# A trunk of two layers on one core: the preparation of mixing weights moved to other steps, operands of the late token sums loaded earlier, and the preparation of query and key weights moved to a later stage

## The chip, the cores and the metric

One core of one Trainium2 chip runs the whole program in one launch. The metric is device time in microseconds (us); lower is better.

## The reference, cut to what matters

The program is a trunk of two layers over 1024 tokens of width 1024, all in fp32. The stage in question is layer 0: a token mixer that joins a gated spatial unit and a gated delta rule, with an output projection, and after it an MLP.

```python
hn = rms_norm(h, ln_mix_e[i])
proj = hn @ w_in_e[i]
a_uv, b_qkv, b_z, b_beta, b_a = jnp.split(proj, split_at, axis=-1)
a_out = gmlp_spatial_gate(jax.nn.gelu(a_uv), gmlp_v_gain[i], gmlp_ws[i], gmlp_bs[i])
b_out = gated_deltanet(b_qkv, b_z, b_beta, b_a, ...)
h = h + jnp.concatenate([a_out, b_out], axis=-1) @ w_out_e[i]
hn = rms_norm(h, ln_mlp[layer])
h = h + jnp.square(jax.nn.relu(hn @ w_mlp1[layer])) @ w_mlp2[layer]
```

`gated_deltanet` splits the tokens into chunks of 64, solves a unit lower triangular system for each chunk and head, and then carries a state through the chunks one after the other (the recurrence). Layer 1 has differential attention with the weights `w_qkv_o` in the mixer's place; those weights are prepared during layer 0.

## The kernel before, in words

**Number format.** Each fp32 operand of a large product is split into two fp32r parts, hi (a cast on ACT) and lo (a subtraction on DVE), and a product is hi·hi + lo·hi + hi·lo: three matmuls (`mm3`). A split of a 128x512 piece is so one ACT cast and one DVE subtraction. Weights pass from DRAM into `raw` slots by SP's queue and are then split.

**Layer 0's mixer** (`even_mix`). Fifteen projections are cut into 384 steps. `pump(n)` runs the steps up to number n between the pieces of the solver and the recurrence, so that TensorE (PE) always has matmuls to do while these wait: steps 108 to 170 beside keys, decay and systems (`system`), 36 beside `solve`, 25 beside `merge`, 29 behind it, and 194 beside the recurrence. What an engine does first is decided when the program is built; on the chip each engine works through its list in order, and an instruction that waits holds up all behind it. That holds for the queues too: SP issues nearly all loads and stores, and POOL those of the preparations.

`solve` (L2292 on) works on DVE: 30 pairs of small operations, `outer` (L2315) and `work` (L2316), and then a transpose that gives `dt` (L2326), in slot "B". The first product that needs it is `py`. The diagonal blocks come in by `work<-diag` and other blocks by `ay<-am_dram`, on SP.

**The output projection** (`mix_seven`, L1669) is one level of a fast scheme with seven products instead of eight: the weight is cut into 2x2 quarters, the tokens' features likewise, and sums of quarters are multiplied. Each product is 48 matmuls of 128x512. The weight combinations are prepared ahead by `prepare_mix` (L300): 28 units, seven for each of four k, each with loads of `w_out`, sums on DVE, a split into a tile `wm` in slot "B", and stores to `mix_dram`. `pump` calls for the next unit at steps after 260 whose number is a multiple of 4 (`BEFORE = 260`). A unit's two stores are held back in a list (`late`) until the next unit begins. Slot "B" is one buffer, so a unit's cast waits until the stores of the unit before have been done.

The token sums are made in `put_ab` (L2167). The first half of the tokens, as it is made, is kept in `halves` in DRAM; for the second half, `halves` is loaded back into temporaries (`tmp`, four buffers) and t1 = first half - second half, t2 = the other quarter - t1 and, later, t4 are made; t2 goes through `t2_dram` (in the trace `t_dram`). t3 (the difference of two quarters) is made at the beginning of `mix_seven` from loads of `halves`. `second_gates` gives the second half's gated values: `guv` is loaded from `uv_dram`, which the last projection steps write; then come the products with the spatial weights (`pgm`), 16 gate operations on DVE (`guv`, L2138) and transposes (`pab`).

Inside `mix_seven`, the third product and the gates come first, then products 1, 5, 6, 7, 2, 4. Finished rows are added to `acc` and stored to `h_dram` by SP (L1706). After product 2's first strip, `rms` (far) sends the reciprocal norms through DRAM: `rd` and then `rb`, a broadcast row, on SP's queue; the normalised operands of the MLP (L1768 to L1773) are made in product 4. `prepare` (L236) makes the query and key weights: 32 units, each with two loads, a cast, a subtraction and two stores to `qk_dram`, all queued on POOL. Five units are called in `mix_seven`, the other 27 in the MLP's second product (`product2`), beside its own products 2, 4, 5 and 7.

The scalar `lame` (in `attn_consts`) comes from a load of `diff_lambda` on SP and an exponential on ACT; it stands between the mixing and the MLP.

## Time and profile before

| | us |
|---|---|
| median of 3 runs | 2576.97 |
| lowest, highest | 2575.22, 2578.17 |
| profiled execution | 2580.56 |
| its span in the trace | 2578.8 |
| PE busy | 2482.0 |
| granted clock of PE, mean | 0.98 |

The profiled execution is 1.8 us longer than its span, and 3.6 us above the median. In the trace, a row of a timeline is start, duration, engine, line, operation, output<-input, and in brackets the idle time before it and what ended it. The chain of waits goes back from the last instruction, each step to what released it. Where a name stands for several buffers, numbers are left out. In the trace, the last matmul of the projections ends at 372.14, the mixing at 525.33, and the MLP's first matmul starts at 551.02.

### The profile page before, as it was taken

How to read it: one execution, taken by the hardware profiler on the slowest of the kernel's cores; microseconds unless marked ns; L12 is line 12 of the kernel's file. 1: busy time of each engine (PE TensorE's matmuls, PEld its weight loads, DVE VectorE, ACT ScalarE, POOL GpSimd, SP SyncE). 2: the span in 40 equal slices, each digit the busy share in tenths (PEclk: the TensorE clock that was granted, in tenths of full speed). 3: DMA queues.
4: the chain of work that ended last, by engine and by line, in shares of the span. 5: the costliest groups of instructions: out<-in, count | busy, mean ns of one | idle time of the engine just before them, and what ended most of it. 6: DMA issues, size and time to landing. Idle time of an engine off the chain costs nothing.

```text
span 2578.8 us, 39762 instructions
## 1 busy us (share of the span) xinstructions
PE 2482.0 (96%) x13369; PEld 2105.7 (82%) x13369; DVE 1888.3 (73%) x3654; ACT 1362.3 (53%) x2768; POOL 378.2 (15%) x491
## 2 busy tenths in 40 slices
PE   9999984869999999999999999999999999999999
PEld 7898983748778888787889999998788888888887
DVE  7877764468886787776795777877788666877676
ACT  5635571246555644563462777765564555445452
POOL 0212441020111120241111233230000000000000
PEclk9999996979999999999999999999999999999999
DMA  8465677655877896798544222266457547756651
GB/s 244 125 182 139 208 241 238 224 181 185 306 266 256 313 326 185 244 314 262 196 135 156 91 67 75 74 217 208 164 188 253 188 168 267 234 182 192 203 176 65
DMA packets 339862, 511.76 MB, mean 198 GB/s; under 512 B 52324, under 2 KB 155720, under 8 KB 339656
## 3 DMA queue, kind: packets, MB, share of 16 engines
q1 hardware_dynamic: 318104, 441.56, 52.7%
q0 software_dynamic: 20992, 67.13, 7.6%
q8 instruction: 105, 1.72, 0.3%
q14 instruction: 101, 0.83, 0.1%
q10 hardware_dynamic: 560, 0.53, 0.1%
HBM read 343.40 MB, written 165.68 MB: 197 GB/s over the span
## 4 chain that ended last, share of the span: by engine, by line
PE 83%; DMA 5%; DVE 5%; issue 4%; ACT 1%; POOL 1%; SPq 0%; DVEq 0%; POOLq 0%; ACTq 0%
PE mm L83 72%; PE po L83 3%; PE qk L83 2%; PE tr L86 2%; PE aux L83 2%; DMA raw<-in_w_mlp_dram 1%; DVE w L375 1%; DMA mix_dram<-wm 1%; DVE raw L449 1%; DMA uv_dram<-t 1%; DMA gate_dram<-w 0%; DMA gd<-g 0%; DVE g L449 0%; DVE lg L1478 0%; DMA t<-halves 0%
## 5 line engine op out<-in xcount | busy, mean ns | idle before, releaser
L83 PE MATMUL mm<-hi,w 128*128 128x512 f32 x1920 | 626.8, 401 | 58.2 <-ACT w L371 25.7
L83 PE MATMUL mm<-g,w 128*128 128x512 f32 x2592 | 601.6, 394 | 3.1 <-DVE g L375 2.5
L83 PEld LDWEIGHTS mm<-g,w 128*128 128x128 f32 x2592 | 486.6, 188 | 116.9 <-DVE g L375 2.9
L371 ACT CAST w<-raw 128x512 fp32r<-128x512 f32 x518 | 315.2, 617 | 373.1 <-PE mm L83 258.8
L83 PEld LDWEIGHTS mm<-hi,w 128*128 128x128 f32 x1920 | 365.4, 191 | 146.8 <-ACT w L371 26.1
L375 DVE TENSOR_TENSOR w<-raw,w 128x512 fp32r<-128x512 f32 x518 | 350.0, 684 | 163.1 <-ACT w L371 126.9
L83 PE MATMUL mm<-w,hi 128*128 128x256 f32 (+2 forms) x2112 | 438.8, 302 | 1.6 <-ACT t L2078 0.8
L83 PE MATMUL mm<-lo,w 128*128 128x512 f32 x960 | 383.9, 400 | 1.7 <-DVE lo L375 1.0
L83 PEld LDWEIGHTS mm<-w,hi 128*128 128x128 f32 x2112 | 339.0, 189 | 18.7 <-DVE k L1388 1.3
L83 PE MATMUL mm<-w,lo 128*128 128x256 f32 (+2 forms) x1056 | 316.2, 300 | 0.0
L83 PE MATMUL mm<-t,w 128*128 128x512 f32 x1152 | 273.2, 396 | 1.9 <-DVE g L449 1.9
L83 PEld LDWEIGHTS mm<-t,w 128*128 128x128 f32 x1152 | 217.6, 189 | 53.0 <-issue 2.4
L83 PEld LDWEIGHTS mm<-lo,w 128*128 128x128 f32 x960 | 183.6, 191 | 44.1 <-DVE lo L375 2.2
L83 PEld LDWEIGHTS mm<-w,lo 128*128 128x128 f32 x1056 | 199.4, 189 | 8.2
L371 ACT CAST g<-graw 128x512 fp32r<-128x512 f32 x216 | 132.9, 617 | 38.0 <-DMA graw<-gd 20.4
L375 DVE TENSOR_TENSOR g<-graw,g 128x512 fp32r<-128x512 f32 x216 | 147.2, 684 | 7.5 <-ACT g L371 3.7
L416 POOL TENSOR_TENSOR r<-ms,mhalf 128x4 f32<-128x4 f32 x12 | 17.2, 1431 | 797.4 <-DVE ms L414 767.1
L1481 ACT ACTIVATE lg<-lg,nm 128x128 f32<-128x128 f32 (+7 forms) x128 | 99.3, 776 | 39.4 <-DVE nm L1478 38.3
L518 ACT ACTIVATE g<-g 128x512 f32<-128x512 f32 x100 | 63.0, 631 | 74.6 <-DVE g L449 74.3
L1478 DVE CUSTOM_DVE_ANT_0 lg<-qk,al 128x512 f32<-128x512 f32 (+3 forms) x128 | 74.1, 586 | 19.1 <-PE qk L83 17.1
L83 PE MATMUL mm<-ohi,w 128*128 128x512 f32 x256 | 83.8, 400 | 0.3 <-DVE acc L1821 0.3
L519 ACT ACTIVATE g<-g 128x512 f32<-128x512 f32 x128 | 80.5, 631 | 2.2
(412 smaller groups left out, 3774.6 us busy)
## 6 DMA issues: line engine op xcount, KB each, us to landing
raw<-in_w_mlp_dram SPq DMA_DIRECT2D x352, 256.0 KB, 3.7
graw<-gd SPq DMA_DIRECT2D x224, 256.0 KB, 3.4
gd<-g SPq DMA_DIRECT2D x192, 256.0 KB, 3.6
acc<-h_dram SPq DMA_DIRECT2D x64, 256.0 KB, 4.7
qk_dram<-w POOLq DMA_DIRECT2D x64, 256.0 KB, 5.5
keep<-in_w_mlp_dram SPq DMA_DIRECT2D x64, 256.0 KB, 5.1
w<-qk_dram SPq DMA_DIRECT2D x64, 256.0 KB, 4.3
raw<-in_w_in_e_dram SPq DMA_DIRECT2D x60, 256.0 KB, 3.8
```

The source lines that it names most:

```text
L83: self._next(self.engine.matmul(*a, **k))
L86: self._next(self.engine.transpose(*a, **k))
L371: inst = self.nc.scalar.copy(hi, src)
L375: inst = (lo_engine or self.nc.vector).tensor_tensor(lo, src, f32(hi), ALU.subtract)
L416: nc.gpsimd.tensor_tensor(r, ms, self.mhalf[:, 0:4], ALU.pow)
L449: nc.vector.tensor_tensor(out, a, b, op)
L518: nc.scalar.activation(g, src, AF.Relu)
L519: nc.scalar.activation(g, g, AF.Square)
L1478: nc.vector.tensor_tensor_reduce(out=lg[:, k0:k1], in0=ps[:, : k1 - k0], in1=al[:, u0 + k0 : u0 + k1], scale=-0.5 ** (hd + 1), scalar=3.0e ...
L1481: nc.scalar.activation(lg[:, :n], lg[:, :n], AF.Exp, bias=nm[:, r, nch - 1 : nch], scale=-1.0, accum_out=me.sums[:, b, r : r + 1])
```

## The change

The units of `prepare_mix` are called at other steps: every eighth from 100 to 188, and every eighth from 240 to 376 (30 calls). Each unit stores its two parts at once in one store of 512 KB. On DVE (`wm` are the units' tiles, `w` those of the projections, `outer` and `work` the solver's) a piece in the middle of the solve was, before:

```order
L2316 TENSOR_TENSOR work_331_1865<-work_331_1865,outer_337_1885 128x11x20
L2315 TENSOR_TENSOR outer_337_1885<-work_331_1865 128x210
L2316 TENSOR_TENSOR work_331_1865<-work_331_1865,outer_337_1885 128x10x21
L2315 TENSOR_TENSOR outer_337_1885<-work_331_1865 128x198
L2316 TENSOR_TENSOR work_331_1865<-work_331_1865,outer_337_1885 128x9x22
L2315 TENSOR_TENSOR outer_337_1885<-work_331_1865 128x184
L375 TENSOR_TENSOR w_352_2096<-raw_350_2093,w_351_2095 128x512
L2316 TENSOR_TENSOR work_331_1865<-work_331_1865,outer_337_1885 128x8x23
L375 TENSOR_TENSOR w_357_2167<-raw_355_2164,w_356_2166 128x512
L2315 TENSOR_TENSOR outer_337_1885<-work_331_1865 128x168
L375 TENSOR_TENSOR w_363_2232<-raw_361_2229,w_362_2231 128x512
```

and is now:

```order
L2313 TENSOR_TENSOR work_344_1915<-work_344_1915,outer_350_1935 128x16x15
L369 TENSOR_TENSOR wm_352_1956<-wm_332_1801,wm_352_1956 128x512
L2312 TENSOR_TENSOR outer_350_1935<-work_344_1915 128x240
L313 TENSOR_TENSOR wm_332_1801<-wm_332_1801,t_351_1954 128x512
L2313 TENSOR_TENSOR work_344_1915<-work_344_1915,outer_350_1935 128x15x16
L313 TENSOR_TENSOR wm_331_1800<-wm_331_1800,wm_332_1801 128x512
L2312 TENSOR_TENSOR outer_350_1935<-work_344_1915 128x238
L2313 TENSOR_TENSOR work_344_1915<-work_344_1915,outer_350_1935 128x14x17
L2312 TENSOR_TENSOR outer_350_1935<-work_344_1915 128x234
L2313 TENSOR_TENSOR work_344_1915<-work_344_1915,outer_350_1935 128x13x18
L2312 TENSOR_TENSOR outer_350_1935<-work_344_1915 128x228
L369 TENSOR_TENSOR wm_358_2031<-t_351_1954,wm_358_2031 128x512
```

Four operations of units stand between the solver's pairs, where the projections' alone stood. From the first `outer` to `dt` there were seven other operations and there are now eighteen.

On POOL (`wm` in DRAM is `mix_dram`, `r`, `rd`, `rb` belong to the norm, `fo`, `rv` to recurrence and gates) the end of the units, the mixing, and what follows was, before:

```order
L307 DMA mix_dram_2840<-wm_649_4091 128x512 x2
L307 DMA mix_dram_2840<-wm_659_4147 128x512 x2
L307 DMA mix_dram_2840<-wm_675_4270 128x512 x2
L307 DMA mix_dram_2840<-wm_680_4320 128x512 x2
L307 DMA mix_dram_2840<-wm_684_4368 128x512
L314 DMA wm_635_4017<-in_w_out_e_dram 128x512
L307 DMA mix_dram_2840<-wm_684_4368 128x512
L307 DMA mix_dram_2840<-wm_690_4415 128x512 x2
L352 DMA mix_dram_2840<-wm_698_4471 128x512 x2
L416 TENSOR_TENSOR r_899_5407<-ms_898_5405,mhalf_89 128x4
L245 DMA raw_917_5479<-in_w_qkv_o_dram 128x2x128 x2
L245 DMA raw_920_5488<-in_w_qkv_o_dram 128x2x128 x2
```

and is now:

```order
L307 DMA mix_dram_1115<-wm_686_4354 128x2x512
L2475 TENSOR_TENSOR fo_733_4608<-so_732_4603,mhalf_89 128x4
L2481 TENSOR_TENSOR qkv_450_2842<-qkv_450_2842,qkv_158_703 128x4x128
L2475 TENSOR_TENSOR fo_808_4957<-so_807_4952,mhalf_89 128x4
L2481 TENSOR_TENSOR qkv_450_2842<-qkv_450_2842,qkv_158_703 128x4x128
L2475 TENSOR_TENSOR fo_850_5177<-so_849_5172,mhalf_89 128x4
L2107 TENSOR_TENSOR rv_666_4166<-var_664_4152,mhalf_89 128x8
L2107 TENSOR_TENSOR rv_670_4206<-var_668_4192,mhalf_89 128x8
L2481 TENSOR_TENSOR qkv_450_2842<-qkv_450_2842,qkv_158_703 128x4x128
L1700 DMA h_dram_93<-acc_741_4658 128x512 x4
L1700 DMA h_dram_93<-acc_832_5039 128x512 x4
L1700 DMA h_dram_93<-acc_802_4888 128x512 x2
```

The last fourteen stores of units stood straight ahead of the norm, with loads of the query and key weights (`in_w_qkv_o`) behind it; now the last unit's store stands ahead of eight operations of recurrence and gates, and stores of `h_dram` come next.

Further: t3 is made in `put_ab` as `halves` is written, with a load of the other quarter, and kept in `t3_dram`; `mix_seven` loads it after product 1. The halves for t1 and t2 are loaded at the beginning of `mix_seven` into free slots of hs tiles (`hi0k`, `lo0k`), and t2 is loaded into slots `c0` to `c3` instead of temporaries. Stores of `h_dram` in `mix_seven` and the norm's `rd` and `rb` go on POOL's queue. All 32 units of `prepare` stand in the MLP's second product: product 7 takes six instead of four, and product 4 eleven instead of eight. What follows is the diff, without the lines that only pass arguments on.

```diff
@@
 KA = (6,5)
 ACC = "A2", "A0", "A1", "A3"
 NQK = 112
-BEFORE = 260
+BESIDE = (*range(100, 190, 8), *range(240, 384, 8))
 MARKS = ((224, NQK),)
 TAIL = 210
 FILLA, FILLB, FILLC, FILLD = 62, 36, 25, 29
@@
 
         nc = self.nc
         self.mix_dram = self.dp.tile([7, 4, 2, P, HT], F32, name="mix_dram")
-        late = []
 
         def put(n, k, src):
-            for out, t in late:
-                nc.gpsimd.dma_start(out, t)
-            late.clear()
             both = self.slot("B", [P, 2, HT], F32R, "wm")
-            for j, t in enumerate(self.split(src, both[:, 0], both[:, 1])):
-                late.append((self.mix_dram[n - 1, k, j], f32(t)))
+            self.split(src, both[:, 0], both[:, 1])
+            nc.gpsimd.dma_start(self.mix_dram[n - 1, k].rearrange("j p m -> p j m"), f32(both))
 
         def get(t, j, l, k):
             nc.gpsimd.dma_start(t, w[(4 * j + k) * P : (4 * j + k + 1) * P, l * HT : (l + 1) * HT])
@@
             if k < 3:
                 x, y = pair(k + 1)
             yield
-        for out, t in late:
-            nc.gpsimd.dma_start(out, t)
 
     def mm3(self, ps, a, b, first, last, more=False):
 
@@
         self.r[half], self.rb[half] = self.rms(half, self.sqs[half], ms, rows, far)
         self.hs[half] = self.hs_new[half]
 
-    def rms(self, half, sqs, ms=None, rows=True, far=False, pt=None):
+    def rms(self, half, sqs, ms=None, rows=True, far=False, pt=None, queue=None):
 
 
         nc = self.nc
@@
         rb = None
         if rows and far:
             d = self.dp.tile([4, P], F32, name=self.nm("rd"))
-            nc.sync.dma_start(d.rearrange("t p -> p t"), r)
+            (queue or nc.sync).dma_start(d.rearrange("t p -> p t"), r)
             rb = self.sp.tile([P, HT], F32, tag=f"rb{half}", name=self.nm("rb"), bufs=1)
-            nc.sync.dma_start(rb, d.rearrange("t p -> (t p)").partition_broadcast(P))
+            (queue or nc.sync).dma_start(rb, d.rearrange("t p -> (t p)").partition_broadcast(P))
         elif rows:
             rb = self.row(half, r)
         return r, rb
@@
             for kt in range(NK):
                 if kt in beside:
                     beside[kt]()
-                if n in (2, 4) and kt % 2 or n == 5 and kt > 2 and kt % 2 or n == 7 and kt in (6, 9, 12, 15):
+                if n in (2, 4) and kt % 2 or n == 5 and kt > 2 and kt % 2 or n == 7 and kt > 4 and kt % 2 or n == 4 and kt in (4, 8, 12):
                     next(side, None)
                 a = self.parts(left(n, kt), nc.vector)
                 raw = self.slot(f"c{next(raws)}", [P, HT], F32, "graw")
@@
             nc.sync.dma_start(h_dram[m, :, cols], res[m])
 
 
-    def mix_seven(self, h_dram, gain_next, gates, halves, t1s, t2s, side):
+    def mix_seven(self, h_dram, gain_next, gates, halves, raws, t1s, t2s, t3_dram):
 
         nc = self.nc
         R = range(4)
@@
             nc.vector.tensor_tensor(t, t, ps, ALU.add)
             if done:
                 self.add_square(h, t)
-                nc.sync.dma_start(h_dram[m, :, h * HT : (h + 1) * HT], t)
+                nc.gpsimd.dma_start(h_dram[m, :, h * HT : (h + 1) * HT], t)
 
         def third():
             a[3] = load(3)
@@
             a[5] = load(5)
 
         a = {}
-        t3s = []
         for k in R:
-            u, v = self.tmp(), self.tmp()
-            nc.sync.dma_start(u, halves[k])
-            nc.sync.dma_start(v, halves[4 + k])
-            nc.vector.tensor_tensor(u, v, u, ALU.subtract)
-            t3s.append(self.split(u, *self.hs_parts(0, k)))
+            for j in range(2):
+                t = self.hp.tile([P, HT], F32, tag=f"{('hi', 'lo')[j]}0{k}", name=self.nm("r"))
+                nc.sync.dma_start(t, halves[4 * j + k])
+                raws[j].append(t)
         for n, _ in enumerate(third()):
             if n > 1:
                 next(gates, None)
@@
             yield from product(q, a[1], self.mixed[1][0:4], x[q], True)
             add(q, 1, x[q])
         a[6] = load(6)
+        t3s = []
+        for k in R:
+            t = self.tmp()
+            nc.sync.dma_start(t, t3_dram[k])
+            t3s.append(self.split(t, *self.hs_parts(0, k)))
         for q in R:
             y = bank("aux")
             yield from product(q, a[5], t1s, y, True)
@@
             y = bank("sc")
             yield from product(q, a[2], self.mixed[1][4:], y, True)
             if q == 0:
-                self.rb[0] = self.rms(0, self.sqs[0], far=True)[1]
+                self.rb[0] = self.rms(0, self.sqs[0], far=True, queue=nc.gpsimd)[1]
             add(q, 1, y, True)
         self.x0 = [acc(m, 0) for m in range(KT)]
-        next(side, None)
-        next(side, None)
         for q in R:
             yield from product(q, a[4], t4s, x[q])
             if q == 0:
@@
                     nc.scalar.copy(hi, t)
                     lows.append(nc.vector.tensor_tensor(lo, t, f32(hi), ALU.subtract).ins.name)
             add(4 + q, 1, x[q], True)
-        for _ in range(3):
-            next(side, None)
         self.sqs_last = self.sqs[1]
         self.x1 = [acc(m, 1) for m in range(KT)]
 
@@
 
         halves = self.dp.tile([KT, P, HT], F32, name="halves")
         t2_dram = self.dp.tile([4, P, HT], F32, name="t2_dram")
-        t1s, t2s = [], []
+        t3_dram = self.dp.tile([4, P, HT], F32, name="t3_dram")
+        t1s, t2s, raws = [], [], ([], [])
         self.t4s = []
 
         def put_ab(hf, k, pt):
@@
                 t = self.tmp()
                 nc.scalar.copy(t, flat(pt))
                 nc.sync.dma_start(halves[k], t)
+                if k < 4:
+                    u = self.tmp()
+                    nc.sync.dma_start(u, halves[4 + k])
+                    nc.vector.tensor_tensor(u, u, flat(pt), ALU.subtract)
+                    nc.sync.dma_start(t3_dram[k], u)
             if hf or k > 3:
                 self.mixed[hf][k] = self.split(flat(pt), *self.hs_parts(hf, k))
             if hf and k < 4:
-                u, v = self.tmp(), self.tmp()
-                nc.sync.dma_start(u, halves[k])
+                u, v = raws[0][k], raws[1][k]
                 nc.vector.tensor_tensor(u, u, flat(pt), ALU.subtract)
                 t1s.append(self.split(u, *self.hs_parts(1, 4 + k)))
-                nc.sync.dma_start(v, halves[4 + k])
                 nc.vector.tensor_tensor(v, v, u, ALU.subtract)
                 t2s.append(self.split(v, *self.hs_parts(0, 4 + k)))
                 nc.sync.dma_start(t2_dram[k], v)
             elif hf:
-                u = self.tmp()
+                u = self.slot(f"c{k - 4}", [P, HT], F32, "t2")
                 nc.sync.dma_start(u, t2_dram[k - 4])
                 nc.vector.tensor_tensor(u, flat(pt), u, ALU.subtract)
                 self.t4s.append(self.split(u, *self.hs_parts(1, k - 4)))
@@
                 done += 1
                 if done % 5 == 0:
                     next(rest_of_x, None)
-                if done > BEFORE and done % 4 == 0:
+                if done in BESIDE:
                     next(parts, None)
             self.pe.fill = False
 
@@
                 T.new_hs()
                 for _ in T.mix_out(0, lambda m: acc_of(m, 0), w_out_o[0], h_dram, gain[4], KA[0]):
                     pass
+            side = iter(()) if layer else T.prepare(w_qkv_o[0])
             if layer:
                 for _ in T.mix_out(1, lambda m: acc_of(m, 1), w_out_o[0], h_dram, gain[4], KA[1]):
                     pass
```

More of the change, by code (lines that the diff above doesn't have):

```diff
@@ L1864, in normed, with even_mix @@
         return a
-    def even_mix(self, first, rows_of_rest, rest_of_x, w_in, ws, bs, conv, a_log, dt_bias, v_gain, o_gain, masks, w_out, gain_next, h_dram, side):
+    def even_mix(self, first, rows_of_rest, rest_of_x, w_in, ws, bs, conv, a_log, dt_bias, v_gain, o_gain, masks, w_out, gain_next, h_dram):
         nc = self.nc
@@ L2492, in mixing @@
             self.new_hs()
-            seven.append(self.mix_seven(h_dram, gain_next, second_gates(), halves, t1s, t2s, side))
+            seven.append(self.mix_seven(h_dram, gain_next, second_gates(), halves, raws, t1s, t2s, t3_dram))
             yield from iter(lambda: next(seven[0]), True)
@@ L2672, in trunk @@
         rest = T.load_x(x1, 1, gain[0], h_dram)
-        side = T.prepare(w_qkv_o[0])
-        T.even_mix(first, rows_of_rest, rest, w_in_e[0], gmlp_ws[0], cols[:, 96:100], conv, gdn_a_log[0], gdn_dt_bias[0], gmlp_v_gain[0], gdn_out_gain[0], masks, w_out_e[0], gain[1], h_dram, side)
+        T.even_mix(first, rows_of_rest, rest, w_in_e[0], gmlp_ws[0], cols[:, 96:100], conv, gdn_a_log[0], gdn_dt_bias[0], gmlp_v_gain[0], gdn_out_gain[0], masks, w_out_e[0], gain[1], h_dram)
         T.attn_consts(attn_q_gain[0], attn_k_gain[0], diff_lambda[0], attn_sub_gain[0], lam_init)
```

## The prediction

> **What bounds the kernel now.** I read the page first. TensorE (PE) is the engine that sets the end:
>
> ```profile
> PE 2482.0 (96%) x13369; PEld 2105.7 (82%) x13369; DVE 1888.3 (73%) x3654; ACT 1362.3 (53%) x2768; POOL 378.2 (15%) x491
> ```
>
> PE works 2482 of 2578.8 us. So only its 97 idle us, and matmuls that run at half clock, can be won; whatever another engine saves while PE is busy is worth nothing. The table by stretches shows where the rest lies (columns: length, then busy us of PE, PEld, DVE, ACT, POOL, the granted clock, the DMA share):
>
> ```profile
> 190.00:372.14 182.14, 178.27 (x1515) 166.94 (x1513) 134.48 (x297) 106.57 (x271) 66.86 (x81) 0.98 0.60 187
> 372.14:411.15 39.01, 18.46 (x85) 14.70 (x85) 17.47 (x43) 15.01 (x35) 9.63 (x13) 0.69 0.84 284
> 411.15:442.81 31.66, 13.05 (x35) 8.18 (x33) 14.32 (x23) 6.79 (x12) 4.85 (x9) 0.57 0.74 238
> 442.81:491.38 48.57, 48.56 (x206) 39.04 (x206) 24.43 (x38) 8.97 (x15) 0.00 (x0) 0.96 0.75 257
> 491.38:525.33 33.95, 25.66 (x104) 20.54 (x104) 11.29 (x19) 6.06 (x10) 6.85 (x9) 0.85 0.44 138
> 525.33:551.02 25.69, 0.00 (x0) 0.00 (x1) 18.88 (x36) 11.37 (x21) 6.14 (x11) 0.56 0.66 230
> ```
>
> I cut it where the timeline of PE shows a boundary: the projections end at 372.14, the first of the late products (a[1]) starts at 411.15, the mixing ends at 525.33, the MLP starts at 551.02. From 372.14 to 551.02 PE is busy 105.7 of 178.9 us: 73 of the 97 idle us lie in this one stage. No other engine is full there either (DVE 17 of 39 us); it is a stage of waits. The timeline of PE and the chain of waits say which:
>
> ```profile
> 371.86 0.28 PE L83 MATMUL mm<-w,lo 128*128 128x256 f32 x1
> ...
> 436.38 0.77 PE L83 MATMUL mm<-hi,w 128*128 128x512 f32 x1 [9.56 <-DVE t L2177]
> ...
> 499.67 0.77 PE L83 MATMUL mm<-hi,w 128*128 128x512 f32 x1 [8.29 <-issue]
> ```
>
> ```profile
> 387.54 7.67 DMA uv_dram<-t
> ...
> 395.60 7.29 DMA guv<-uv_dram
> ...
> 440.01 2.76 DMA w<-mix_dram
> ...
> 480.28 11.11 PE mm L83 x48
> ...
> 499.67 6.20 PE mm L83 x16
> ```
>
> First comes a round trip of the last uv tile through memory (15 us), then loads of `halves` for the t1 operands, then the load of the last `mix_dram` unit (440.01 to 442.77). At 436.38 PE waited 9.56 us behind a subtraction that a load of `halves` held up; at 499.67 it waited 8.29 us for the t2 loads. The 48 matmuls in 11.11 us give the price of one product, 0.2315 us a matmul; the 16 matmuls in 6.20 us after the pause at 499.67 should have taken 3.70, so a restart costs 2.5 us of half clock beside the wait. The Trainium skill ("TensorE: Matmul & The Clock Gate", Part 1: The HAM clock gate) says that full clock comes back after some 3.4 us of activity; by that a restart costs 1.7 us, not 2.5, and the two restarts in the sum below would make it 1.6 us lower. The row shows the longer half-rate stretch.
>
> **The change part by part.** *The mixing, from 372.14 to 525.33 (153.2 us).* The order shows that all 28 units are stored before it, that the t1 raws are loaded into slots of their own, t3 is formed while `halves` is written, and t2 is loaded into a free slot. So the waits at 436.38 (9.56), for `mix_dram` (to 442.77) and at 499.67 (8.29) have nothing left to wait for. What is late next is the chain uv store, guv load, 16 gate multiplications, transposes: it ends where a[1] starts, 39.0 us after the projections' end, and the change does not touch it, except that its two transfers (7.67 and 7.29 us, at a DMA share of 0.84) lose the company of seven stores and loads of units. With these at some 4.5 to 5 each I get a[1] at 34 us after the end of the projections; unhelped, 39; if the load waits longer behind the new loads in SP's queue, 50. Then six products of 48 matmuls at 11.11 us: 66.7. The transposes of the second half and the sum matmuls: 2.6. One restart: 2.5. Small waits that I can't name: 4 (0 to 10). Sum 34 + 66.7 + 2.6 + 2.5 + 4 = 109.8, against 153.2: **a gain of 43**. Ends: 50 + 66.7 + 2.6 + 2.5 + 10 = 132, a gain of 21; 30 + 66.7 + 2.6 + 2.5 + 0 = 102, a gain of 51.
>
> *The start of the MLP (25.69 us of wait).* Here are the DVE and SP rows:
>
> ```profile
> 522.75 1.42 DVE L1768 SCALAR_TENSOR_TENSOR acc<-acc,cols,rb 128x512 f32<-128x512 f32 x2 [11.01 <-DMA rb<-rd]
> ...
> 549.04 0.22 DVE L1326 TENSOR_TENSOR t<-t 128x64 f32<-128x64 f32 x1 [6.23 <-DMA t<-in_diff_lambda_dram]
> ```
>
> ```profile
> 508.01 0.37 SPq L420 DMA_DIRECT2D rd<-r x1
> 518.34 0.32 SPq L422 DMA_DIRECT2D rb<-rd x1
> ...
> 539.58 0.99 SPq L1324 DMA_DIRECT2D t<-in_diff_lambda_dram x1
> ```
>
> The reciprocal norms `rb` come 14.7 us after `rd` is issued; the first weights come late because SP stood behind stores of `h_dram`, and ACT's casts stood behind a scalar that waits for `diff_lambda` until 549. After the change the `h_dram` stores are on POOL, the five units of `prepare` with their loads and stores are gone from here, and the MLP's raw loads follow the mixing's on SP at once. PE has 67 matmuls left after the sums of squares (15.5 us), and from `rd` to the first multiplication it is 14.7 again, with an estimated 2 for mean and reciprocal in front of it and 2 for the first cast and subtraction behind: a wait of 3. Then PE is fed tile by tile by DVE and ACT, which share the eight normalised tiles with the first weights; I put 6 us of gaps there, 1.5 for `diff_lambda`, 0.5 for the clock: 11, against 25.7 + 2.5 (the clock after 551.02, as at 499.67): **a gain of 17** (9 to 24). The Trainium skill ("Trainium Kernel Development and Optimization", Key Constraints) says that queues of SP, ACT and POOL share 16 DMA engines, so that another issuer saves only issue time; by it the move of `rd`, `rb` and the stores to POOL brings `rb` no earlier, and the rows agree: between `rd` and `rb` SP waited 10 us for a transfer. My sum takes nothing for that move.
>
> *The solve, where units now are.* The change puts twelve calls of the preparation at steps 100 to 188, where before there were none. The rows:
>
> ```profile
> 158.65 0.21 DVE L2315 TENSOR_TENSOR outer<-work 128x30 f32<-128x30 f32 x1 [1.35 <-DMA work<-diag]
> ...
> 176.86 0.68 DVE L375 TENSOR_TENSOR w<-raw,w 128x512 fp32r<-128x512 f32 x1
> ...
> 184.19 2.12 DVE L2326 STREAM_TRANSPOSE dt<-work 128x1024 f32<-128x1024 f32 x1
> ```
>
> ```profile
>   DVE dt L2326: 0.4, 1
> ```
>
> ```profile
> 150.78 1.06 SPq L2297 DMA_DIRECT2D work<-diag  x2
> 151.88 3.63 SPq L2301 DMA_DIRECT2D ay<-am_dram  x4
> ```
>
> The single row in the middle is PE's wait at `py`, the first product with the solver's result: 0.4 us, so PE arrives just as `dt` is ready, and the amount of matmuls ahead of it is the same in both orders. Every us that `dt` comes later is idle PE. Before, seven other operations stand between the first outer product and `dt`; after, 18 do: 11 x 0.60 (the starts of neighbouring 0.68 us rows are 0.6 apart) = 6.6. In front of the solve, where DVE has no pause, four more unit operations: 2.4; two of the four `ay` loads now precede `work<-diag` on SP: up to 1.8, I take 1. A unit's cast waits until the last unit's store has landed, because all share slot B; in the solve two units are nine rows apart, about 4.4 us of work:
>
> ```profile
> mix_dram<-wm POOLq DMA_DIRECT2D x56, 256.0 KB, 3.5
> ```
>
> With issue, landing and cast that is 4.7 us or more, so DVE itself waits 0.3 to 3 us at two places: 1.0 in all as the value, 6 as the bound. PE's restart adds 2.5. Sum 6.6 + 2.4 + 1 + 1 + 2.5 = 13.5; **a loss of 13** (4 if DVE's gaps take the units up, 20 with all bounds). The store is one of 512 KB where two of 256 KB were; the trace has no such store, and 3.5 and twice 3.5 us bound its landing. A unit also puts POOL's two AFFINE_SELECTs for the next system behind a store that waits for DVE; I take nothing for it beside the unit operations already counted, since the same order on DVE holds both up, and one landing, 3.5 us, as the other end. In the recurrence (190.00 to 372.14) DVE is busy 134 of 182 us, and 18 calls stand there now where 30 stood before, so I take zero.
>
> *The second product pass.* Five units of `prepare` more stand beside products 7 and 4:
>
> ```profile
> 1057.00:1102.00 45.00, 41.93 (x180) 33.45 (x179) 35.07 (x58) 28.13 (x52) 15.89 (x25) 1.00 0.84 287
> 1146.00:1190.00 44.00, 43.34 (x192) 35.00 (x191) 31.26 (x52) 22.95 (x42) 13.53 (x21) 1.00 0.94 289
> ```
>
> A unit moves 0.75 MB: 2.6 us at 287 GB/s. Two more fit in product 7 (16% of 45 us is free); three more (7.9 us) exceed the 2.6 us free in product 4, and 5 us would be late if nothing were loaded ahead: **a loss of 2** (0 to 6).
>
> *The sum*, against the profiled execution's 2580.6 (span 2578.8 and 1.8 around it): 2580.6 - 43 - 17 + 13 + 2 = 2535.6. That execution lay 3.6 above the median of the runs, so I forecast **2532**.
>
> **The rivals.** *A, the waits move (0.17).* The guv load stands in SP's queue behind loads that wait for slots, and the mixing still ends on memory round trips as in the chain's rows (7.67 and 7.29). For it: they are untouched. Against: the other loads have their data ready. a[1] then starts at +50 and other waits remain: the gain of 43 is 21, the time 2554.
> *B, the MLP's start stays bound (0.10).* `diff_lambda` is issued even later on SP, behind the raws, and ACT's casts stand behind it as until 549.04. The 9.5 us from its issue to its use come back, the time 2541.
> *C, the solve hides the units (0.08).* DVE catches up before `py`, so 4 instead of 13, and the mixing gains 51 and the MLP's start 24: 2508.
> *D, slower (0.05).* Each unit's cast waits for the previous store, and ACT and DVE stand still with it, being in order. If that costs 3.5 us at each of the seven units around the solve (24.5) and at each of the 18 units in the recurrence (63, of which the 48 us of DVE's free time there would hide at most a part, say 10), the loss is 24 + 53 and the net gain is gone: 2532 - 13 + 24.5 + 53 = 2596. It decides from about 1.8 us a unit on top of my sum (45 us / 25 units). Against it: before, more units stood in the recurrence, and PE is busy 178 of 182 us there.
> That the units do not leave the mixing is no rival: the order shows it.
>
> **How the numbers follow.** My own case has 0.60. A measurement of this kernel can tell 0.2%, 5 us, from no change; that is 2571.8 to 2582.1. My case and B and C lie wholly below it, A to all but a few per cent, D above: faster 0.93, same 0.02, slower 0.05. The likeliest gives 2532. The mixing at its bounds alone makes it 2524 to 2554; the solve and the MLP's start at theirs add 16 below and 15 above, the second pass 4 above. They do not all fall on one side, so my case alone has some 2512 to 2556. With C's 2508 and A's 2554, which have their own spread, the range is **2505 to 2560**; D and the outer parts of A and C are left out.
>
> **What the profile would show.** The three PE waits at 436, 442 and 499 gone, and PE near 10 of 10 from a[1] to the mixing's end; the stretch from the projections' end to a[1] 30 to 39 us; mixing 102 to 132 in all; the MLP's first matmul 3 to 15 us after it; a new wait of PE at `py` of about 11 us with `dt` as its releaser and half clock after it; product 4 within 6 us of before. I am wrong if `py` shows no wait or one over 20 us, if PE idles in the recurrence behind `wm` casts, or if a[1] starts over 45 us after the projections.

## The result, and the profile after

The changed kernel takes 2534.27 us, median of 4 runs (2529.96 to 2535.88), against 2576.09 (2568.98 to 2578.17): ratio 0.984, 95% interval 0.9817 to 0.9863. The forecast was 2532 in a range of 2505 to 2560. The profiled execution has a span of 2532.8 us, 46.0 less than before; by the medians it is 41.8, since the profiled execution of the kernel before was a long one. The page after, in its first part and in the row of the late products:

```profile
PE 2478.3 (98%) x13369; PEld 2105.5 (83%) x13369; DVE 1889.8 (75%) x3654; ACT 1361.2 (54%) x2768; POOL 375.7 (15%) x481
...
L83 PE MATMUL mm<-hi,w 128*128 128x512 f32 x1920 | 622.5, 400 | 8.6 <-DMA w<-gate_dram 3.6
```

The number of matmuls is the same; 58.2 us of idle time in front of this group have become 8.6. The stretches of the changed kernel, cut where its PE timeline shows the same boundaries as before (py, the projections' end, the first product a[1], the mixing's end), with columns as before:

```profile
0.00:198.39 198.39, 183.58 (x1163) 164.51 (x1163) 156.11 (x347) 106.92 (x265) 43.60 (x49) 0.99 0.72 215
198.39:392.09 193.70, 187.25 (x1648) 174.66 (x1648) 134.42 (x291) 109.35 (x277) 57.85 (x59) 0.95 0.59 182
392.09:431.81 39.72, 25.71 (x115) 21.07 (x115) 14.44 (x37) 8.88 (x23) 1.40 (x2) 0.79 0.84 296
431.81:501.47 69.66, 69.65 (x314) 56.49 (x312) 42.97 (x70) 21.65 (x36) 8.94 (x15) 1.00 0.71 233
```

The fourth row is the main gain: from a[1] on, PE is busy 69.65 of 69.66 us at full clock, where the same products took 114.2 us before. And the PE timeline shows what is left of waits over 2 us between 100 and 520:

```profile
198.39 1.81 PE L83 MATMUL py<-dt,ay 32*32 32x32 f32 x60 [10.66 <-DVE dt L2323]
246.49 0.33 PE L86 MATMUL pq<-ident,qkv 128*128 128x128 f32 x1 [2.50 <-DVE qkv L2004]
...
405.19 2.08 PE L83 MATMUL pgm<-guv,wT 128*128 128x128 f32 x8 [3.48 <-DVE t L2169]
426.05 3.78 PE L83 MATMUL pgm<-guv,wT 128*128 128x128 f32 x16 [7.62 <-DVE guv L2131]
504.76 0.80 PE L83 MATMUL mm<-hi,w 128*128 128x512 f32 x1 [3.30 <-ACT hi L1767]
```

The waits for the t1 and t2 operands and for `mix_dram` are gone. The wait at `py` is new, with `dt` as its releaser, as foreseen; the wait for `guv` (426.05) has stayed. The stages of all kernels, in us, as the PE timelines give them (the projections' end is the end of the last 128x256 matmul; the rest is the span behind the MLP's first matmul):

| kernel | projections' end | to a[1] | to the mixing's end | MLP's wait | rest |
|---|---|---|---|---|---|
| before | 372.1 | 39.0 | 114.2 | 25.7 | 2027.8 |
| changed | 392.1 | 39.7 | 69.7 | 3.3 | 2028.0 |
| units alone | 390.2 | 29.5 | 81.3 | 24.1 | 2022.1 |
| units late | 379.0 | 44.0 | 97.9 | 4.8 | 2030.3 |
| operands back | 394.1 | 28.3 | 81.0 | 6.5 | 2024.4 |
| prepare back | 391.3 | 39.2 | 69.7 | 20.3 | 2024.2 |
| not in the solve | 393.7 | 39.2 | 69.6 | 3.7 | 2026.4 |
| t3 in slots | 390.4 | 32.2 | 69.9 | 3.6 | 2031.6 |
| slots and no call | 395.0 | 31.2 | 69.9 | 4.5 | 2024.9 |
| SP queue | 392.3 | 37.4 | 69.7 | 2.3 | 2028.1 |
| units on POOL | 393.2 | 36.4 | 69.7 | 3.9 | 2026.8 |
| two stores | 384.4 | 37.3 | 69.7 | 3.8 | 2029.1 |
| slots and SP queue | 390.5 | 32.4 | 70.1 | 2.2 | 2029.8 |
| three edits | 386.2 | 31.8 | 69.9 | 2.3 | 2032.0 |

So 46.0 = 114.2 - 69.7 (44.5) + 25.7 - 3.3 (22.4), less 19.9 at the projections' end, 0.7 to a[1] and 0.2 in the rest. Kernels with one code up to the projections' end (changed, prepare back, SP queue, and but for one slot t3 in slots) differ there by 1.9 us, and the rest, whose code hardly differs, by 10; so a few us are read from the stages and not from the spans.

### The profile page after: what moved, and what is told of

Its sections match the earlier page's. It is cut to its first block, busy times and chain, and to the rows that moved or that the text cites. A ratio compares the mean times of both kernels' runs of the same rounds, so it can differ in the third digit from the quotient of the medians.

```text
span 2532.8 us, 39684 instructions
## 1 busy us (share of the span) xinstructions
PE 2478.3 (98%) x13369; PEld 2105.5 (83%) x13369; DVE 1889.8 (75%) x3654; ACT 1361.2 (54%) x2768; POOL 375.7 (15%) x481
## 4 chain that ended last, share of the span: by engine, by line
PE 82%; issue 5%; DMA 5%; DVE 4%; ACT 1%; POOL 1%; SPq 0%; POOLq 0%; DVEq 0%; ACTq 0%
PE mm L83 72%; PE qk L83 2%; PE po L83 2%; PE tr L86 2%; PE aux L83 2%; DMA mix_dram<-wm 1%; DMA wm<-in_w_out_e_dram 1%; DMA w<-gate_dram 1%; DVE lg L1472 0%; DVE t L2001 0%; DMA t<-halves 0%; DMA t<-in_p_dram 0%; DVE w L369 0%; POOL gate_dram L258 0%; DMA diag<-ring 0%
## 5 line engine op out<-in xcount | busy, mean ns | idle before, releaser
L365 ACT CAST g<-graw 128x512 fp32r<-128x512 f32 x216 | 132.9, 617 | 22.4 <-DMA graw<-gd 7.8
L1475 ACT ACTIVATE lg<-lg,nm 128x128 f32<-128x128 f32 (+7 forms) x128 | 99.2, 776 | 38.5 <-DVE nm L1472 37.4
```

The costliest lines, as they stand in the source:

```text
L365: inst = self.nc.scalar.copy(hi, src)
L1475: nc.scalar.activation(lg[:, :n], lg[:, :n], AF.Exp, bias=nm[:, r, nch - 1 : nch], scale=-1.0, accum_out=me.sums[:, b, r : r + 1])
```

## The experiments

**Which part of the change does it.** Four kernels, run together. The first two move the units alone.

```diff
-BESIDE = (*range(100, 190, 8), *range(240, 384, 8))
+BESIDE = tuple(range(264, 384, 4))
```

> The changed kernel with the units called at the steps of before (every fourth from 264 on), each still with one store. My theory: PE's wait at py (10.66 us) goes and the projections end near 372 instead of 392, but the last units are stored some 50 us into the mixing and PE waits for mix_dram again; about 25 us come back there: near 2540 us (2530 to 2555). Rival, the operands loaded ahead are the whole gain and late units cost nothing: 20 us are won, 2514.

Measured: 2553.04, ratio 0.9912 (0.9893 to 0.9931), 19 us slower than the changed kernel. The direction is my theory's and the time lies in its range, but the size is larger than the value that I gave:

```profile
448.46 0.79 PE L83 MATMUL mm<-hi,w 128*128 128x512 f32 x1 [14.12 <-DMA w<-mix_dram]
```

PE waits 14.12 us at one place for a unit's weights. There is no wait at `py`. But the projections end at 379.0, not at 372, though the steps are those of before: 7 us that I come back to at the two stores.

The kernel before, with the units' new steps and the one store, and nothing else:

```diff
-                if done > BEFORE and done % 4 == 0:
+                if done in BESIDE:
```

> The kernel before with the units' steps and the one store of the changed kernel, and nothing else. My theory: it pays the 20 us in the solve and the recurrence, and gains only the waits for mix_dram (5.7 and 3.5 us) and some transfer time in the mixing, 10 to 15: near 2583 us (2575 to 2592), not faster than before. Rival, the units in the mixing were most of its waits: 25 us faster, 2550.

Measured: 2549.33, ratio 0.9897 (0.9879 to 0.9915): 26 us faster. My theory fell, the rival's number is met. In this kernel t1 and t2 are loaded as before, and the PE timeline shows

```profile
198.71 1.49 PE L83 MATMUL py<-dt,ay 32*32 32x32 f32 x48 [10.63 <-DVE dt L2319]
...
414.59 3.46 PE L83 MATMUL pgm<-guv,wT 128*128 128x128 f32 x16 [4.64 <-DVE guv L2131]
475.59 0.77 PE L83 MATMUL mm<-hi,w 128*128 128x512 f32 x1 [7.15 <-DVE t L2179]
525.05 0.79 PE L83 MATMUL mm<-hi,w 128*128 128x512 f32 x1 [24.08 <-ACT w L364]
```

The price at `py` is whole. But the 9.56 us behind a subtraction of t1 (436.38 before) are gone with the units, with no load ahead. In before's DVE list these subtractions stood among the units' operations, in order, and waited for slow loads:

```profile
431.44 0.69 DVE L2180 TENSOR_TENSOR t<-t,t 128x512 f32<-128x512 f32 x1 [6.40 <-DMA t<-halves]
432.05 0.68 DVE L375 TENSOR_TENSOR wm<-wm,wm 128x512 fp32r<-128x512 f32 x1
432.77 0.69 DVE L317 TENSOR_TENSOR wm<-wm,wm 128x512 f32<-128x512 f32 x1
435.55 0.69 DVE L2177 TENSOR_TENSOR t<-t,pab 128x512 f32<-128x512 f32 x1 [2.09 <-DMA t<-halves]
```

Put the other way round, the kernel with late units, which has all of the change but the moved steps, is some 23 us faster than before by its ratio; the two parts, 26 and 23, bring 41 together and so overlap. Whether the units held the subtractions by their place in DVE's list, by the temporaries that they take from the same ring, or by their transfers was not separated. What remains with the old loads are the 7.15 us for t2 at 475.59.

The changed kernel with the token sums' operands as before:

```diff
-                u, v = raws[0][k], raws[1][k]
+                u, v = self.tmp(), self.tmp()
+                nc.sync.dma_start(u, halves[k])
...
+                nc.sync.dma_start(v, halves[4 + k])
...
-                u = self.slot(f"c{k - 4}", [P, HT], F32, "t2")
+                u = self.tmp()
```

(and t3 again at the start of the mixing)

> The changed kernel with the token sums' operands loaded as before (halves into temporaries for t1 and t2, t3 made at the start of the mixing, t2 through temporaries). My theory: the waits for halves and t2 come back as they were, 9.6 + 8.3 and some 5 of half clock and small ones: near 2557 us (2547 to 2565). Rival, without the units' stores the same loads land in time: 2540 or less.

Measured: 2537.47, ratio 0.9845 (0.9824 to 0.9865), 1 us from the changed kernel and within its interval. My theory fell. The stages say why: the late products are 11 us longer (81.0, with 7.41 us of wait for t2), the MLP's wait 3 us, but a[1] comes 28.3 us behind the projections' end instead of 39.7. What the early loads win is lost again in front; that t3's temporaries take most of it is shown below, with t3 in slots.

The changed kernel with `prepare` where it was:

```diff
+        next(side, None)
+        next(side, None)
         for q in R:
             yield from product(q, a[4], t4s, x[q])
...
+        for _ in range(3):
+            next(side, None)
```

> The changed kernel with five units of queries and keys back in the mixing. My theory: their loads, casts and stores stand before the MLP's first weights again, and the wait at the MLP's start grows from 3.3 to 13 to 18 us: near 2547 us (2541 to 2552). Rival, the stores of h_dram on SP were what held the weights: no change, 2534.

Measured: 2543.91, ratio 0.9871 (0.9851 to 0.9891), 8 us slower by the ratios. The theory holds. The wait at the MLP's start is 20.27 us, more than the 13 to 18 expected, and part of it comes back behind, where the normalised tiles and weights then lie ready: in the 25 us from the MLP's first matmul on, PE does 105 matmuls here and 88 in the changed kernel, which is 4 us.

**Where t3's cost sits.** In the changed kernel the last gelu of the projections (ACT, L2071) and the load of `guv` read

```profile
407.27 0.84 ACT L2071 ACTIVATE t<-mm,r 128x256 f32<-128x256 f32 x2 [7.72 <-DMA halves<-t]
```

```profile
416.64 0.89 SPq L1684 DMA_DIRECT2D w<-mix_dram  x2
417.58 0.50 SPq L2120 DMA_DIRECT2D guv<-uv_dram  x1
```

The gelu has its matmuls long since, and waits for one of the four temporaries, of which t3 now takes one more per k; `guv` follows it.

```diff
                 if k < 4:
-                    u = self.tmp()
+                    u = self.slot(f"c{k}", [P, HT], F32, "t3")
```

> The changed kernel with the t3 operands in slots c0 to c3 instead of the four temporaries. The last gelu waited 7.72 us for a temporary that a store of halves held, and the load of guv follows it. My theory: that wait goes and the first product after the gates starts 30 to 34 us after the projections' end instead of 39.7: near 2527 us (2523 to 2530). Rival, the transfers, at 365 to 400 GB/s in that stretch, set the end anyway: 2533 or more.

Measured: 2526.90, ratio 0.9819 (0.9804 to 0.9833), and a[1] at 32.2 us instead of 39.7. As expected. The transfers did not set the end at 39.7.

**What the projections lose.** No call in the solve:

```diff
-BESIDE = (*range(100, 190, 8), *range(240, 384, 8))
+BESIDE = (*range(100, 160, 8), *range(208, 384, 8))
```

> The changed kernel with no call at steps 164 to 188 and four more at 208 to 232, so that one unit operation instead of seven stands in the solve. My theory (DVE's own operations in the solve make dt late): PE's wait at py falls from 10.66 to 2 to 4 us and its restart goes: 10 to 12 us faster than the changed kernel, near 2523 us. First rival, the operations in front of the solve make it late: 4 us, 2530. Second rival, the units at 208 to 232 hold up the merge as much: 2534.

Measured: 2538.34, ratio 0.9863 (0.9847 to 0.9879), not faster. The wait at `py` did fall:

```profile
191.77 3.62 PE L83 MATMUL py<-dt,ay 32*32 32x32 f32 x128 [4.24 <-DVE dt L2323]
222.52 1.11 PE L86 MATMUL pv<-ident,qkv 128*128 128x128 f32 x4 [4.98 <-ACT yt L2381]
248.33 0.48 PE L86 MATMUL pq<-ident,qkv 128*128 128x128 f32 x1 [3.44 <-DVE qkv L2004]
```

but a wait of 4.98 us behind `yt` took its place, and ACT shows what `yt` waited for:

```profile
221.88 0.59 ACT L2381 COPY yt<-py 128x512 f32<-128x512 f32 x1 [2.61 <-DMA mix_dram<-wm]
```

`yt` waits for a unit's store to land: the merge puts `yt` into slot B, which the units use. The second rival holds. With t3 in slots as well:

> The edits of the two kernels before the last together: no units at steps 164 to 188, t3 in slots. My theory: the gains add, 11 + 7: near 2516 us (2510 to 2524). Rival, what is won in the solve is lost again in the mixing, because the transfers set its pace: no better than the better of the two alone.

Measured: 2528.56, ratio 0.9824 (0.981 to 0.9838), no better than t3 in slots alone, as its rival said; the projections end at 395.0. That the transfers are the reason is not shown: the kernel without calls in the solve had gained nothing by itself that could have been added.

Next, the units' arithmetic on POOL, with nothing else moved:

```diff
-            self.split(src, both[:, 0], both[:, 1])
+            self.split(src, both[:, 0], both[:, 1], nc.gpsimd)
...
-            nc.vector.tensor_tensor(out, a, b, op)
+            nc.gpsimd.tensor_tensor(out, a, b, op)
```

> The changed kernel with the units' 44 sums and subtractions on POOL instead of DVE; loads, casts, stores, slot and steps as they are. A like operation of POOL (L2040) takes 1.30 us. My theory: the 20 us between the start and the projections' end are DVE's time, so they shrink to about 10, with PE's wait at py at 4 to 6 instead of 10.66: near 2524 us (2519 to 2529). Rival, the chain through slot B and the queues that wait in order make it late, whichever engine subtracts: the wait at py stays near 10 us, 2533 or more.

Measured: 2531.18, ratio 0.984 (0.9826 to 0.9853), as the changed kernel; the projections end at 393.2. The forecast fell: 44 operations were taken off DVE, and the projections' end came no earlier. Two waits of PE take the place of the one:

```profile
188.43 1.22 PE L83 MATMUL mm<-hi,w 128*128 128x512 f32 x2 [5.10 <-DVE w L369]
203.57 3.62 PE L83 MATMUL py<-dt,ay 32*32 32x32 f32 x128 [6.75 <-DVE dt L2323]
```

The ACT timeline shows one thing that changed:

```profile
177.83 0.62 ACT L365 CAST wm<-wm 128x512 fp32r<-128x512 f32 x1 [6.63 <-DMA mix_dram<-wm]
183.51 0.62 ACT L365 CAST wm<-t 128x512 fp32r<-128x512 f32 x1 [2.78 <-DMA mix_dram<-wm]
189.04 0.62 ACT L365 CAST wm<-wm 128x512 fp32r<-128x512 f32 x1 [3.65 <-DMA mix_dram<-wm]
```

ACT, in order, stands for the previous unit's store, 13 us in the solve, where it stood 6 in the changed kernel; the projections' weight casts stand behind it. DVE's timeline shows another, beside a subtraction of POOL:

```profile
178.54 1.41 POOL L369 TENSOR_TENSOR wm<-wm,wm 128x512 fp32r<-128x512 f32 x1 [6.28 <-ACT wm L365]
```

```profile
178.39 0.41 DVE L2313 TENSOR_TENSOR work<-work,outer 128x238 f32<-128x238 f32 x1
178.83 1.38 DVE L2312 TENSOR_TENSOR outer<-work 128x234 f32<-128x234 f32 x1
180.24 0.40 DVE L2313 TENSOR_TENSOR work<-work,outer 128x234 f32<-128x234 f32 x1
```

Seven of the solver's sixty operations took 1.33 to 1.89 us, where like ones take 0.33 to 0.41, and each ended 0.2 to 0.3 us behind a subtraction of POOL that ran beside it. The sixty took 27.4 us in all, against 19.8 in the changed kernel, and from the first `outer` to the end of `dt` it is 40.8 us instead of 34.6. So POOL's subtractions cost the solve more of DVE's time than they took off it, and this kernel decides neither for my theory nor for the chain through slot B. The third try shortens that chain and leaves the arithmetic where it is:

```diff
-            self.split(src, both[:, 0], both[:, 1])
-            nc.gpsimd.dma_start(self.mix_dram[n - 1, k].rearrange("j p m -> p j m"), f32(both))
+            for j, t in enumerate(self.split(src, both[:, 0], both[:, 1])):
+                nc.gpsimd.dma_start(self.mix_dram[n - 1, k, j], f32(t))
```

> The changed kernel with two stores of 256 KB a unit, one behind the other, instead of one of 512 KB. My theory: it moves the landing by less than 1 us and costs POOL 0.6 us of issue a unit: 2533 to 2537, no difference that can be measured. Rival, the single large store lands later and holds slot B: 3 to 5 us faster with two, 2530.

Measured: 2526.12, ratio 0.9824 (0.9811 to 0.9838), and the projections end at 384.4, 7.7 us earlier than in the changed kernel where like code differs by 1.9. The rival holds in its direction; the times alone, 4 us apart by the ratios, have intervals that overlap. The store's landing, the changed kernel first, then two stores:

```profile
mix_dram<-wm POOLq DMA_DIRECT2D x28, 512.0 KB, 4.3
```

```profile
mix_dram<-wm POOLq DMA_DIRECT2D x56, 256.0 KB, 3.2
```

and the waits for `wm` summed up, that for the landed store and DVE's for the cast, first in the changed kernel:

```profile
  DMA mix_dram<-wm: 21.3, 8
...
  DVE wm L369: 24.8, 12
```

and with two stores

```profile
  DMA mix_dram<-wm: 13.7, 7
...
  DVE wm L369: 13.0, 8
```

The hi part leaves as soon as ACT has made it, while DVE still subtracts; the one store waits for both and takes 1.1 us more to land. Whether the earlier start or the shorter landing counts more was not separated. In PE's own terms, `py` starts at 196.32 instead of 198.39; from there to the projections' end PE idles 6.4 us in both kernels, but is busy 181.65 us with two stores and 187.25 in the changed kernel, for the same 1648 matmuls, at a mean granted clock of 0.98 and 0.95. So 2.1 of the 7.7 us are the earlier `py`, and the others are time at half clock that did not come; how much of these belongs to the stores is open. A second pair of kernels that differ by the two stores, the last two below, puts the projections' end 4.3 us apart. Nor is it shown that the one store accounts for the 7 us of the kernel with late units: its casts waited 45.8 us for landed stores, those of before 49.4, and two stores were not tried there.

**The queue.** Stores of `h_dram`, `rd` and `rb` back on SP:

```diff
-                nc.gpsimd.dma_start(h_dram[m, :, h * HT : (h + 1) * HT], t)
+                nc.sync.dma_start(h_dram[m, :, h * HT : (h + 1) * HT], t)
...
-                self.rb[0] = self.rms(0, self.sqs[0], far=True, queue=nc.gpsimd)[1]
+                self.rb[0] = self.rms(0, self.sqs[0], far=True)[1]
```

> The changed kernel with the stores of h_dram and the norm's rd and rb back on SP's queue. My theory: the MLP's raw loads stand behind stores that wait for DVE, and the first weights come later: the wait at the MLP's start grows from 3.3 to about 10 us, near 2541 us. Rival, the queue only saves issue time, and the units of queries and keys were what held the weights: 2534 to 2535.

Measured: 2529.74, ratio 0.9831 (0.9818 to 0.9845): not slower; the intervals don't separate it from the changed kernel. The theory fell. From the mean of squares to the first use of `rb`, DVE shows in the changed kernel

```profile
485.94 0.15 DVE L408 TENSOR_SCALAR ms<-aux 128x4 f32<-128x4 f32 x1
...
503.25 1.41 DVE L1763 SCALAR_TENSOR_TENSOR acc<-acc,cols,rb 128x512 f32<-128x512 f32 x2 [11.05 <-DMA rb<-rd]
```

and with the SP queue

```profile
483.83 0.15 DVE L408 TENSOR_SCALAR ms<-aux 128x4 f32<-128x4 f32 x1
...
498.98 1.42 DVE L1763 SCALAR_TENSOR_TENSOR acc<-acc,cols,rb 128x512 f32<-128x512 f32 x2 [10.21 <-DMA rb<-rd]
```

17.3 us on POOL's queue, 15.2 on SP's. Over all kernels the same stretch took 15.0 to 16.1 us in the five with the SP queue and 15.6 to 18.0 in the nine with POOL's. The raw loads did not suffer on SP. The Trainium skill ("DMA: Bandwidth & Descriptors", Specifications) puts the first byte at about 1 us on GpSimd's path and 0.6 on SP's, an estimate of 0.8 for two transfers in a row; these two traces have the same sign and a larger difference, in a stretch that holds more than the two transfers.

**What comes out on top.** Slots and SP queue together, then with two stores:

> The changed kernel with t3 in slots c0 to c3 and with the stores of h_dram and the norm's rd and rb on SP, the two edits that were each faster than the changed kernel. My theory: they touch different waits and add up, 7 + 4: near 2523 us (2519 to 2526). Rival, the second only was faster by chance or because a[1] came earlier: 2527, as the slots alone.

Measured: 2525.60, ratio 0.9818 (0.9805 to 0.9832), between theory and rival, which lie too close to be told apart.

> The changed kernel with three edits together: two stores of 256 KB a unit, t3 in slots c0 to c3, and the stores of h_dram with rd and rb on SP. My theory: the two stores shorten the chain through slot B before the projections' end (6 to 8 us), the slots and the queue act behind it (8), so they add: near 2519 us (2515 to 2523). Rival, what the earlier end of the projections wins is lost to transfers in the mixing: 2525, as without the two stores.

Measured: 2521.73, ratio 0.9804 (0.9788 to 0.9821): the lowest median of all, some 9 us below the changed kernel by the ratios; its interval overlaps that of slots and SP queue. The projections end at 386.2, a[1] follows after 31.8, the MLP's wait is 2.3: all three gains are in the stages, 5.9 + 7.9 + 1.0, less 4.0 in the rest. The wait of 9.38 us at `py` is still there.

## Why the prediction was right, point by point

The total was right, 2532 against 2534, and that it came so near is in part luck: the solve with the recurrence lost 7 us more than the sum has, and what lies behind the mixing gained 7 us more. Within the mixing, too, two parts missed by 6 us, one each way.

- **The mixing, a gain of 43.** Measured 153.2 - 109.4 = 43.8. But its parts were not: a[1] came at 39.7, not 34 (and just outside the 30 to 39 that I named as a sign), and the products behind it took 69.7, not 75.8, since no small waits were left. The 34 rested on two transfers that would fall to 4.5 to 5 us each; the load of `guv` (417.58) took 7.26, against 7.29 before. The step "the waits at 436.38, for `mix_dram` and at 499.67 have nothing left to wait for" holds for the result. For `mix_dram` it also holds for the reason given: with late units that wait is back (14.12). For the first it does not: the units alone take it away. The loads ahead were needed only for t2 (7 us), which t3's temporaries then cost at `guv`. Of rival A, the guv load behind others in SP's list, a piece was there; the temporary in front of it was the larger, and I had not seen it.
- **The start of the MLP, a gain of 17.** The wait is 3.3; I had said 3, and 8 more of gaps, `diff_lambda` and clock behind it. Some 4.4 of these came: in the 25 us from the MLP's first matmul on, PE does 88 matmuls, where it did 107 before, and 19 matmuls are 4.4 us at 0.2315. So the start gave 22.4 - 4.4 = 18.0. `prepare` is the cause of most of the wait, as shown by putting it back (20.3). The move to POOL's queue brought nothing, as the sum took it.
- **The second pass, a loss of 2.** At the end of product 4 PE now waits 1.20 and 1.98 us for weights from `gate_dram`, about what I expected; but a wait of 2.49 us in product 7, at 1069.28 before, is gone, so the pass loses nothing. Two waits that the sum did not look at, 1.08 us at 690.53 and 1.94 at 753.01 before, are gone too. Together the rest is only 0.2 longer, and 22.2 were won where the two terms gave 15.
- **The solve, a loss of 13.** Measured 19.95, the term that was mis-sized. The wait at `py` is 10.66 (11 expected). The solve itself was well worked out: it starts 5.1 later (163.71 against 158.65; I had 3.4) and is 7.0 longer to the end of `dt` (7.6 expected). My reading that DVE's operations make it longer holds there: the solver's own sixty took 19.8 us, as before (19.9), DVE waited only 1.5 us for casts, and with the units' calls taken out the solve is 27.8 us long, as before (27.7). The step that failed is "so I take zero" for the recurrence: from `py` to the projections' end it is 193.7 instead of 185.7 us, with 2.6 more idle and 5.4 more of busy time for the same matmuls, by a lower granted clock. Of these 8.0 us, 2.5 were in the sum as the restart. I had also not seen that operations moved out of the solve would cost as much in the merge.
- **Half clock.** A restart was put at 2.5 us from 499.67. After the 10.66 us at `py`, the windows show the granted clock at 0.50 until 204 and 0.58 until 207:

```profile
198.00:201.00 3.00, 2.61 (x98) 2.61 (x100) 2.80 (x3) 2.46 (x4) 0.68 (x2) 0.50 0.03 5
201.00:204.00 3.00, 3.00 (x43) 2.55 (x40) 0.72 (x2) 1.88 (x4) 0.36 (x1) 0.50 0.00 0
204.00:207.00 3.00, 3.00 (x10) 2.34 (x9) 0.69 (x1) 2.95 (x5) 0.00 (x0) 0.58 0.00 0
207.00:210.00 3.00, 3.00 (x109) 2.46 (x109) 1.05 (x2) 2.95 (x6) 0.00 (x0) 1.00 0.00 0
```

That is 8.1 us of half rate from 198.39 on, so about 4 us lost at this one restart. The wait of 2.50 at 246.49 is followed by 0.62 and 0.53 in the windows from 247 to 249 and to 251, and after waits of 1.26, 1.08 and 0.83 us near 315 the clock is at 0.50 to 0.69 until 323, some 3.4 us more. With two stores PE idles as long in that stretch (3.2 us from 310 to 330), and the clock stays at 1.00; what makes it fall after waits this short is not shown. The Trainium skill ("TensorE: Matmul & The Clock Gate", Part 1: The HAM clock gate) has full clock back after some 3.4 us of activity; here the half rate lasted 8.1 us from 198.39, and before 4.9 from 499.67.
- **Rival D** was in the recurrence in small: PE waited some 2.6 us more there, far from the 53 that it needed. B (the MLP bound by `diff_lambda`) did not come: no wait of PE stands behind it. C did not either: the wait at `py` is there in full.

## What to carry to other kernels

Background work in a single buffer is a chain over all engines that touch it: each piece waits for the landing of the one before, and engines that work in order make other work wait with it. Sending each part when it is made shortened that chain here. Moving the arithmetic to an idle engine did not help, and the trace has to be read for the engine that was to be relieved: its operations had become longer. A temporary taken from a shared ring for an early load can hold up an operation on the critical path; ask of every new buffer who is next in its ring. And where several waits share a stage, undo the parts of a change one by one before giving each its gain: here the part that looked like the cure was worth 1 us as it was built, and some 7 once t3 had slots of its own, and moving the work beside it 26.

## What the runs showed of the hardware that was not expected

One store of 512 KB from a pair of tiles landed 4.3 us after its issue (median), two of 256 KB each 3.2, both on POOL's queue, for the same 28 units. A subtraction of 128x512 took 1.294 us on POOL and 0.69 on DVE; beside such subtractions on POOL, seven of the solver's operations on DVE took 1.33 to 1.89 us instead of 0.33 to 0.41. After 10.66 us of idle time the half-rate stretch was 8.1 us long, after 8.29 us it was 4.9. The stretch around the two small transfers `rd` and `rb` took 17.3 us with POOL's queue and 15.2 with SP's in the pair of kernels above.
